# Batched 64 x 64 matmul: four of the casts of b go from VectorE to ScalarE

## The chip, the cores and the metric

The kernel runs on one core of a Trainium2 chip. The core has TensorE (PE in the profile), VectorE (DVE), ScalarE (ACT), GpSimd (POOL) and SyncE (SP), which run their own instruction streams and meet at semaphores, and 16 DMA engines which serve the queues of SyncE (q1), ScalarE (q10) and GpSimd (q0). The metric is the device time of one execution in microseconds.

## The reference

```python
def setup_inputs():
    return {
        "a": np.random.randn(1024, 64, 64).astype(np.float32),
        "b": np.random.randn(1024, 64, 64).astype(np.float32),
    }

def reference(a: np.ndarray, b: np.ndarray) -> np.ndarray:
    return np.matmul(a, b).astype(np.float32)
```

There are 1024 independent products of 64 x 64 matrices in fp32. Each of a, b and the output has 16.8 MB, so a run reads 33.55 MB and writes 16.78 MB of HBM.

## The kernel before, in words

The batch is cut into 16 tiles t of 64 products. A tile of b (`b_sb`, 128 partitions x 16 x 128, fp32) is 1 MB. a is loaded for two tiles at once, as a super-tile s = t // 2. Each tile goes through these steps:

- `load_b(t)` brings the fp32 tile of b to SBUF. Odd tiles are issued by ScalarE, even tiles by SyncE (L97). There are three buffers, so the load of tile t + 3 can only be issued when the cast of tile t has read its buffer. In the loop `load_b(t + 3)` stands in iteration t, just after `cast(t + 1)`.
- `cast(t)` turns the tile into bf16 (`b_bf`, two buffers). This is L173. Tile 0 is cast by ScalarE, tiles 1 to 14 by VectorE, tile 15 in quarters by both (L178, L180).
- a is loaded by `load_a`: three quarters of a super-tile are converted to bf16 by GpSimd's DMA (`a_sb`, L74) and the fourth comes as fp32 through SyncE (`a_raw`, L78). Its transposition is made by VectorE for super-tiles 2 to 5 (`transpose_dve`: L128, with ScalarE casting `a_raw` at L126), and by TensorE for the others (`transpose`: L138, evacuated by ScalarE at L141, after VectorE's `regroup` at L109 and L112).
- `spread(t)` copies the transposed a into a block-diagonal tile (`at_bd`, two buffers) on VectorE: eight copies at L154 or four at L164.
- `multiply(t)` runs 64 matmuls (L218) into two PSUM tiles (`o_ps`, two buffers, one for each half of t). ScalarE copies each half out with four instructions (L206), eight for a tile. For tiles 11 and 13 VectorE takes two of these eight, and for the last tile half of its copies.
- `store(t)` writes the 1 MB of products from GpSimd's queue (L195), for the last two tiles from SyncE's and ScalarE's.

The work is written out by hand under `tc.manual_schedule()`: on each engine the instructions stand in the order of the program text. In iteration t of the main loop that order is: `spread(t + 1)`, `cast(t + 1)`, `load_b(t + 3)`, `load_a` (some iterations), TensorE transposes of the second half (some), `multiply(t)` with its copies, then the regroup or the transposition of a super-tile further on, and the store of tile t - 1. On ScalarE this means, for even t: whatever iteration t - 1 left (copies of t - 1, the cast of `a_raw` or transposed copies), then `load_b(t + 3)`, then the copies of product t.

Below, "cast 7" is `cast(7)`, "load b9" is `load_b(9)`, "copies 6" are the copies from PSUM of `multiply(6)`.

Of the kernel before, what the change touches and what calls it, by code (L numbers as in the profile page):

```python
# [13 lines left out]
def kernel(  # L14
# [14 lines left out]
    nc = tc.nc  # L29
# [7 lines left out]
    N_BD = 2  # L37
    HOLD = 2
    ON_DVE = (2, 3, 4, 5)

    a_v = a.rearrange("(s g h) (mp v) k -> s h g mp (v k)", h=4, g=32, v=16)
    b_v = b.rearrange("(t g h) (kp u) n -> t (h kp) g (u n)", h=4, g=16, u=2)
# [27 lines left out]
    def load_a(s):  # L70

        a_sb = a_pool.tile([128, 3, 16, 64], bf16, name="a_sb")
        for h in range(3):
            nc.gpsimd.dma_start(  # L74
                out=a_sb[:, h, :, :].rearrange("p v k -> p (v k)"), in_=a_v[s, h], single_packet=True
            )
        a_raw = a_pool.tile([128, 16, 64], fp32, name="a_raw")
        nc.sync.dma_start(out=a_raw[:].rearrange("p v k -> p (v k)"), in_=a_v[s, 3])  # L78
        a_tiles[s] = a_sb, a_raw
# [53 lines left out]
    def transpose(s, j):  # L133
        a_cols = abf_tiles[s][:].rearrange("p v h k -> p v (h k)").bitcast(fp32)
        for wl in range(2):
            at_ps = t_psum.tile([128, 4, 128], fp32, name="at_ps")
            for vo in range(4):
                nc.tensor.transpose(  # L138
                    at_ps[:, vo, :], a_cols[:, 4 * vo + 2 * j + wl, :], identity[:]
                )  # L140
            nc.scalar.copy(  # L141
                at_tiles[s][:, :, 2 * j + wl, :, :],
                at_ps[:].rearrange("p vo (g mp) -> p g mp vo", mp=4),
            )

    def spread(t):
        bd = bd_tiles[t % N_BD]
        at_sb = at_tiles[t // 2]
        for h in range(4):
            rows = slice(32 * h, 32 * h + 32)  # L150
            if t // 2 in ON_DVE:
                for i in range(2):
# [16 lines left out]
    def cast(t):  # L169
        b_bf = work.tile([128, 16, 128], bf16, name="b_bf")  # L170
        b_sb = b_tiles.pop(t)
        if t < n_t - 1:
            (nc.vector.tensor_copy if t else nc.scalar.copy)(b_bf[:], b_sb[:])  # L173
        else:
            for gq in range(4):
                rows = slice(4 * gq, 4 * gq + 4)
                if gq % 2:
                    nc.vector.tensor_copy(b_bf[:, rows, :], b_sb[:, rows, :])  # L178
                else:
                    nc.scalar.copy(b_bf[:, rows, :], b_sb[:, rows, :])  # L180
        bbf_tiles[t] = b_bf
# [5 lines left out]
    def multiply(t):  # L187
# [20 lines left out]
        for half in range(2):  # L208
# [19 lines left out]
            if not last:  # L228
                copies = [nc.scalar.copy] * 4
                if half and t % 2 and t > 2 * max(ON_DVE):  # L230
                    copies[2:] = [nc.vector.tensor_copy] * 2
# [7 lines left out]
    with tc.manual_schedule():  # L239
# [15 lines left out]
        transpose(0, 1)  # L255
        spread(0)
        cast(0)
        for t in range(n_t):
            s, half = t // 2, t % 2
            if t + 1 < n_t:  # L260
                spread(t + 1)
                cast(t + 1)
            if t + B_AHEAD < n_t:
                load_b(t + B_AHEAD)
            if half == 0 and 0 < s < n_s - 1 - A_AHEAD:
                load_a(s + 1 + A_AHEAD)
            if half == 0 and 0 < s < n_s - 1 and s + 1 not in ON_DVE:
                transpose(s + 1, 1)
            multiply(t)
            if t == 0:  # L270
                regroup(1)
                load_a(A_AHEAD)
                load_a(A_AHEAD + 1)
                transpose(1, 0)
                transpose(1, 1)
            if t and s + 2 in ON_DVE and (half or s):
                for part in [0, 1] if t == 1 else [half]:
                    transpose_dve(s + 2, part)
                if half:
                    a_tiles.pop(s + 2)  # L280
            elif half == 0 and 0 < s and s + 2 < n_s:
                regroup(s + 2)
            elif half == 1 and s + 2 < n_s:
                transpose(s + 2, 0)
            if t >= HOLD - 1:
                store(t - HOLD + 1)
# [32 lines left out]
```

## Time and profile before

| | |
|---|---|
| time, median of 3 runs | 134.24 us (134.1 to 134.47) |
| time of the profiled execution | 134.24 us |
| its span, from first to last instruction | 132.1 us |
| VectorE busy | 100.7 us (76%) |
| ScalarE busy | 89.2 us (68%) |
| TensorE matmul busy | 63.2 us (48%) |
| moved between HBM and SBUF | 381 GB/s over the span |

The page of the profile divides the span into 40 slices of 3.3 us. The rows of tenths give for each slice the busy share of an engine as a digit (9 is 90% or more). A group line names the source line, the engine, the operation, output and input, and the number of instructions, then the busy time and the mean duration in ns, then the idle time of the engine just before them with what ended it. A timeline line gives the start, the duration and the instruction; a bracket tells how long the engine was idle before it and what it waited for. `ACTq` marks the issue of a DMA. In the DMA view an issue line ends with the time from issue to landing, and a queue line gives packets, MB and the share of the 16 engines' time. (The "0.5 KB" of a b load's issue line is not its size; a load has 1 MB.)

### The profile page before, as it was taken

The numbers are of one execution on the slowest core, as the hardware profiler recorded it, in microseconds if no ns is written. First come the engines' busy times: TensorE is split into PE (matmuls) and PEld (weight loads), VectorE is DVE, ScalarE is ACT, GpSimd is POOL, SyncE is SP. The second block draws the span as 40 slices with busy tenths as digits, with TensorE's granted clock in tenths as the row PEclk, the third lists the DMA queues.
The fourth block names the chain that finished last, engine by engine and source line by source line (L and its number), as shares of the span: only waits on it lengthen the run. The fifth ranks groups of instructions, "written<-read, shape, count | busy, mean of one in ns | idle before, by whom it ended". The sixth has DMA issues, their size and how long they took to land.

```text
span 132.1 us, 2719 instructions
## 1 busy us (share of the span) xinstructions
PE 63.2 (48%) x1088; PEld 60.5 (46%) x1088; DVE 100.7 (76%) x150; ACT 89.2 (68%) x159; POOL 32.0 (24%) x43
## 2 busy tenths in 40 slices
PE   0006406990733701909190737359709834677700
PEld 0006306980733701909190737259709734676700
DVE  5930399209999915999989998999999998598730
ACT  2225524999893790583989197929999996728970
POOL 8991000420074000702061302040203040312000
PEclk9999999999686555555555555555995995555555
DMA  3999999999999999999999999999999999999996
GB/s 83 351 336 310 309 313 277 288 301 327 326 305 385 371 308 298 395 385 396 327 282 357 402 395 347 296 326 387 399 392 394 394 392 387 398 399 396 364 324 201
DMA packets 19020, 44.99 MB, mean 341 GB/s; under 512 B 1088, under 2 KB 3136, under 8 KB 19008
## 3 DMA queue, kind: packets, MB, share of 16 engines
q0 software_dynamic: 6832, 20.19, 50.6%
q1 hardware_dynamic: 7120, 14.68, 30.8%
q10 hardware_dynamic: 5056, 9.96, 20.0%
q8 instruction: 8, 0.13, 0.4%
q14 instruction: 4, 0.03, 0.1%
HBM read 33.55 MB, written 16.78 MB: 381 GB/s over the span
## 4 chain that ended last, share of the span: by engine, by line
DMA 37%; DVE 27%; ACT 13%; PE 9%; issue 8%; ACTq 2%; SPq 1%
DMA b_sb<-in_b_dram 31%; DVE at_bd L154 11%; ACT o_sb L206 11%; DMA o_sb<-in_a_dram 6%; DVE b_bf L173 6%; PE o_ps L218 5%; DVE at_bd L164 4%; PE at_ps L138 3%; DVE at_sb L128 3%; DVE a_bf L109 1%; DVE a_bf L112 1%; ACTq L97 1%; ACT a_bf L126 1%; ACT a_bf L106 1%; ACT at_sb L141 1%
## 5 line engine op out<-in xcount | busy, mean ns | idle before, releaser
L206 ACT COPY o_sb<-o_ps 64x512 f32<-64x512 f32 x116 | 67.4, 581 | 19.2 <-PE o_ps L218 16.1
L218 PEld LDWEIGHTS <-at_bd 128*128 128x128 bf16 x1024 | 50.5, 125 | 52.9 <-DVE b_bf L173 44.7
L218 PE MATMUL o_ps<-b_bf,at_bd 128*128 128x64 bf16 x960 | 49.1, 231 | 49.4 <-DVE b_bf L173 42.7
L164 DVE COPY at_bd<-at_sb 32x1024 f32<-32x1024 f32 x32 | 23.2, 724 | 12.7 <-ACT at_sb L141 11.9
L154 DVE COPY at_bd<-at_sb 32x512 f32<-32x512 f32 x64 | 27.9, 436 | 1.3
L195 POOL DMA_DIRECT2D out_dram<-o_sb x14 | 15.5, 1108 | 47.5 <-ACT o_sb L206 30.7
L74 POOL DMA_DIRECT2D a_sb<-in_a_dram x21 | 12.4, 606 | 39.8 <-DVE at_sb L128 26.4
L173 DVE CAST b_bf<-b_sb 128x2048 bf16<-128x2048 f32 x14 | 17.2, 1227 | 6.4 <-DMA b_sb<-in_b_dram 6.0
L138 PE MATMUL at_ps<-identity,a_bf 128*128 128x128 f32 x64 | 11.2, 349 | 11.2 <-ACT a_bf L106 11.2
L138 PEld LDWEIGHTS at_ps<-identity,a_bf 128*128 128x128 f32 x64 | 10.3, 188 | 11.1 <-issue 11.1
L128 DVE STREAM_TRANSPOSE at_sb<-a_sb 128x512 f32<-128x512 f32 x12 | 12.0, 1062 | 0.0
L141 ACT COPY at_sb<-at_ps 128x512 f32<-128x512 f32 x16 | 8.5, 594 | 2.1 <-PE at_ps L138 2.0
L106 ACT CAST a_bf<-o_sb 128x1024 bf16<-128x1024 f32 x2 | 2.1, 1044 | 5.2 <-DMA o_sb<-in_a_dram 5.2
L128 DVE STREAM_TRANSPOSE at_sb<-a_bf 128x512 f32<-128x512 f32 x4 | 4.2, 1053 | 0.7 <-ACT a_bf L126 0.7
L126 ACT CAST a_bf<-a_raw 128x1024 bf16<-128x1024 f32 x4 | 4.2, 1046 | 0.7 <-DMA a_raw<-in_a_dram 0.6
L173 ACT CAST b_bf<-b_sb 128x2048 bf16<-128x2048 f32 x1 | 1.9, 1898 | 3.7 <-DMA b_sb<-in_b_dram 3.7
L206 DVE COPY o_sb<-at_ps 64x256 f32<-64x256 f32 x8 | 3.4, 422 | 1.3 <-PE at_ps L218 1.2
L246 DVE MEMSET at_bd<- 128x4096 f32 x1 | 3.5, 3472 | 0.8 <-issue 0.8
L218 PE MATMUL at_ps<-b_bf,at_bd 128*128 128x64 bf16 x64 | 3.6, 242 | 1.0 <-DVE at_bd L164 1.0
L106 DVE CAST a_bf<-o_sb 128x1024 bf16<-128x1024 f32 x2 | 2.8, 1385 | 1.7 <-DMA o_sb<-in_a_dram 1.7
L206 ACT COPY o_sb<-at_ps 64x256 f32<-64x256 f32 x8 | 2.9, 367 | 0.1
L180 ACT CAST b_bf<-b_sb 128x512 bf16<-128x512 f32 x2 | 1.1, 616 | 2.8 <-DMA b_sb<-in_b_dram 2.8
(16 smaller groups left out, 15.4 us busy)
## 6 DMA issues: line engine op xcount, KB each, us to landing
out_dram<-o_sb POOLq DMA_DIRECT2D x14, 1024.0 KB, 21.1
a_sb<-in_a_dram POOLq DMA_DIRECT2D x21, 256.0 KB, 16.0
a_raw<-in_a_dram SPq DMA_DIRECT2D x7, 512.0 KB, 16.9
o_sb<-in_a_dram SPq DMA_DIRECT2D x2, 512.0 KB, 5.8
o_sb<-in_a_dram ACTq DMA_DIRECT2D x2, 512.0 KB, 7.1
out_dram<-o_sb SPq DMA_DIRECT2D x2, 512.0 KB, 3.6
out_dram<-o_sb SPq DMA_DIRECT2D x2, 256.0 KB, 3.6
out_dram<-o_sb ACTq DMA_DIRECT2D x2, 256.0 KB, 3.1
```

The source lines that it names most:

```text
L74: nc.gpsimd.dma_start(out=a_sb[:, h, :, :].rearrange("p v k -> p (v k)"), in_=a_v[s, h], single_packet=True)
L106: copy(a_bf[:, :, h, :], a_sb[h].rearrange("p (v k) -> p v k", v=16))
L126: nc.scalar.copy(rows, raw[:])
L128: nc.vector.transpose(at_tiles[s][:, h].rearrange("p g w mp vo -> p w vo g mp"), pairs.rearrange("p (vo w kp) -> p w vo kp", vo=4, w=4),)
L138: nc.tensor.transpose(at_ps[:, vo, :], a_cols[:, 4 * vo + 2 * j + wl, :], identity[:])
L141: nc.scalar.copy(at_tiles[s][:, :, 2 * j + wl, :, :], at_ps[:].rearrange("p vo (g mp) -> p g mp vo", mp=4),)
L154: nc.vector.tensor_copy(bd[rows, 8 * i : 8 * i + 8, :, h, :, :].rearrange("p g w mp vo -> p (g w) (mp vo)"), at_sb[block : block + 32, h]. ...
L164: nc.vector.tensor_copy(bd[rows, :, :, h, :, :].rearrange("p g w mp vo -> p (g w) (mp vo)"), at_sb[rows, half].rearrange("p g w mp vo -> p ...
L173: (nc.vector.tensor_copy if t else nc.scalar.copy)(b_bf[:], b_sb[:])
L195: store_queue(t, lo).dma_start(out=o_v[t, :, lo : lo + n, :], in_=o_sb[:, lo : lo + n].rearrange("p gh j wl n -> p (gh j wl n)"),)
L206: copies[2 * par + wl](dst, src)
L218: nc.tensor.matmul(o_ps[:, gl, g % 2, j, :], at_bd[:, j, g, :, u], b_bf[:, g, 64 * u : 64 * u + 64], start=(u == 0), stop=(u == 1),)
```

## The change

ScalarE casts the b tiles 5, 7, 9 and 11 besides tile 0; VectorE casts the other tiles up to 14. The place of `cast` in the program text stays, so on ScalarE's stream the cast of tile t + 1 stands ahead of `load_b(t + 3)` and of the copies of product t, for t = 4, 6, 8 and 10. Buffers, queues and the rest are as before.

```diff
--- before.py
+++ after.py
@@ -37,6 +37,7 @@
     N_BD = 2
     HOLD = 2
     ON_DVE = (2, 3, 4, 5)
+    ON_ACT = (0, 5, 7, 9, 11)
 
     a_v = a.rearrange("(s g h) (mp v) k -> s h g mp (v k)", h=4, g=32, v=16)
     b_v = b.rearrange("(t g h) (kp u) n -> t (h kp) g (u n)", h=4, g=16, u=2)
@@ -170,7 +171,7 @@
         b_bf = work.tile([128, 16, 128], bf16, name="b_bf")
         b_sb = b_tiles.pop(t)
         if t < n_t - 1:
-            (nc.vector.tensor_copy if t else nc.scalar.copy)(b_bf[:], b_sb[:])
+            (nc.scalar.copy if t in ON_ACT else nc.vector.tensor_copy)(b_bf[:], b_sb[:])
         else:
             for gq in range(4):
                 rows = slice(4 * gq, 4 * gq + 4)
```

## The prediction

> **What bounds the kernel now.** b5 means b tile 5, and so on; times are us from the span's start. I read the page first, then ScalarE's and VectorE's timelines, then the DMA view cut to single issues.
>
> ```profile
> DVE  5930399209999915999989998999999998598730
> ACT  2225524999893790583989197929999996728970
> DMA  3999999999999999999999999999999999999996
> ...
> L173 DVE CAST b_bf<-b_sb 128x2048 bf16<-128x2048 f32 x14 | 17.2, 1227 | 6.4 <-DMA b_sb<-in_b_dram 6.0
> ...
> L173 ACT CAST b_bf<-b_sb 128x2048 bf16<-128x2048 f32 x1 | 1.9, 1898 | 3.7 <-DMA b_sb<-in_b_dram 3.7
> ```
>
> From 50 to 112 us VectorE is full, ScalarE has holes until 89, and the DMA engines are full almost throughout: three limits lie close together. One cast takes 1.227 us on VectorE and 1.898 on ScalarE. So by engine time alone the change pays: 4 x 1.227 = 4.9 us off VectorE, 4 x 1.898 = 7.6 onto ScalarE (89.2 to 96.8 of 132.1).
>
> What decides is when the tiles land. The loads of odd tiles are issued by ScalarE (L97). Issue and time to landing, from the DMA view cut to one issue each (first two lines: b7 issued at 52.49, b9 at 66.04; then b11 at 80.16, b13 at 94.00, b15 at 104.84):
>
> ```profile
> b_sb<-in_b_dram ACTq DMA_DIRECT2D x1, 0.5 KB, 16.6
> b_sb<-in_b_dram ACTq DMA_DIRECT2D x1, 0.5 KB, 16.9
> b_sb<-in_b_dram ACTq DMA_DIRECT2D x1, 0.5 KB, 14.7
> b_sb<-in_b_dram ACTq DMA_DIRECT2D x1, 0.5 KB, 15.6
> b_sb<-in_b_dram ACTq DMA_DIRECT2D x1, 0.5 KB, 14.4
> ```
>
> Landings: b7 69.1, b9 82.9, b11 94.9, b13 109.6, b15 119.2; b5 51.3 (35.18 + 16.1). VectorE's casts began at 58.31, 72.37, 86.13 and 97.80 for 5, 7, 9, 11: 3 to 7 us after landing. Now ScalarE around the place of cast 7 and load b9:
>
> ```profile
> 65.98 0.02 ACT L97 MOVE_SHAPE b_sb<-in_b_dram  x1
> 66.04 0.70 ACTq L97 DMA_DIRECT2D b_sb<-in_b_dram  x1
> 66.28 1.05 ACT L126 CAST a_bf<-a_raw 128x1024 bf16<-128x1024 f32 x1
> 67.93 4.74 ACT L206 COPY o_sb<-o_ps 64x512 f32<-64x512 f32 x8 [0.60 <-PE o_ps L218]
> 75.58 4.74 ACT L206 COPY o_sb<-o_ps 64x512 f32<-64x512 f32 x8 [2.91 <-PE o_ps L218]
> ```
>
> b9 was issued at 66.04, 0.09 after VectorE's cast 6 (64.72 + 1.23) released its buffer, three us before b7 landed. The new cast 7 stands before that issue in ScalarE's program. Does a waiting cast hold the issue behind it? Once in this trace, yes:
>
> ```profile
> 35.02 1.05 ACT L126 CAST a_bf<-a_raw 128x1024 bf16<-128x1024 f32 x1 [0.60 <-DMA a_raw<-in_a_dram]
> 35.12 0.02 ACT L97 MOVE_SHAPE b_sb<-in_b_dram  x1
> 35.18 0.70 ACTq L97 DMA_DIRECT2D b_sb<-in_b_dram  x1
> ```
>
> b5's buffer was free from 33.94 (cast 2), but its issue came only once the cast ahead, which waited for its own data, had begun.
>
> Last, a load's delay is not only transfer. ScalarE's ring (q10) in the microsecond from 70, the first that lists it after the issue at 66.04:
>
> ```profile
> q0 software_dynamic: 59, 0.17, 52.8%
> q1 hardware_dynamic: 58, 0.12, 32.4%
> q10 hardware_dynamic: 42, 0.09, 22.1%
> ```
>
> Likewise 52.49 to 56.5 and 80.16 to 84.3: some 4.1 us from issue to first packet. Rings with work get equal packet counts (48 to 50 per us with three rings, 67 with two), and a load is 512 packets of 2 KB.
>
> **The change, part by part.**
>
> *Removed.* Four casts leave VectorE. Cast 5 gives all it promises: spread 5 ends at 58.28, so matmul 5 starts at 58.3 instead of 59.6. The later ones are limited by ScalarE, below.
>
> *Cast 5 on ScalarE.* ScalarE is done with the a_raw cast at 49.6, b5 lands at 51.3, the cast runs to 53.2. Load b7 behind it waits for cast 4 (52.41) anyway, and copies 4 (the evacuation of product 4) start at 54.39. ScalarE's own hole before 54.39 hides it, at no cost; had b5 landed at 54.4 instead, copies 4 would start 1.9 late.
>
> *Cast 7.* Copies 5 now end at 65.0 and a_raw at 66.1, then ScalarE waits for b7 until 69.1 and casts to 71.0. Behind it stand load b9 (66.04 becomes 69.2) and copies 6 (67.93 becomes 71.0, to 75.7). Who waits for those: matmul 7, whose first PSUM half is free at 73.4 against its start at 73.66 before. So VectorE's 1.2 to 2.4 us of lead are used up here, and what is left is a load issued 3.2 us later.
>
> *Cast 9.* b9 lands at 69.2 + 16.9 = 86.1 (own row of before, with three rings again sharing); copies 8 start at 88.0 instead of 82.05, copies 9 end at 97.5 instead of 94.1, and load b11 is issued at 86.2 instead of 80.16.
>
> *Cast 11.* Before, b11 had SyncE's ring empty beside it for part of its transfer. Now b12, issued near 88, shares most of the way, as b14 did with b13; so b13's 15.6 is the nearest row, and b11 lands at X = 86.2 + 15.6 = 101.8 (94.9 before). Bounds: 14.4 and 16.9 for both loads give X = 98.1 to 103.1. ScalarE is free at 98.5 (copies 9, two transposed copies of 0.51), so the landing is what ends last.
>
> *From X to the end.* ScalarE then has cast 11 (1.9), two transposed copies (1.0), copies 10 (4.75), copies 11 (3.6), half a us more, then load b15: X + 11.7 = 113.5, where it was 104.84. VectorE's spread 12 waits for those transposed copies and cast 12 ends near 109, in time. b15's time to land: 14.4 in its own row, where b14 and a store shared the way. Below: 4.1 to the first packet, 1.05 MB at the 400 GB/s of full windows (2.6), 1.4 from last packets to landing, 8.1 in all. I take 11.0, since b14 will be through and one store (256 packets of 4 KB at 67 per us, 4 us) runs beside it. b15 lands at 124.5. From its landing to the end the trace of before has 132.1 - 119.2 = 12.9, and this part is ScalarE's (cast 1.1, copies 14 4.75, copies 15 3.0, last store 3.3 and 0.7), so it stays: 137.4. ScalarE's own work from X + 11.3 (four transposed copies 2.05, copies 12 4.75, copies 13 3.6) makes it free at X + 21.7 = 123.5, so the wait for b15 is 1.0, and with no wait at all the end would still be X + 34.6 = 136.4.
>
> *Queues moved past.* SyncE's loads b8, b10, b12, b14 are released by casts 5, 7, 9, 11: 59.6 to about 54, 73.7 to 71.0, 87.4 to 88.0, 99.1 to 103.7. The first two only queue behind a_raw loads on the same ring. b14 with the 16.1 of its row lands at 119.8, in time for copies 14 at 125; if it took 20 it would cost. GpSimd's stores follow the copies: 8, 9, 10 go at 93, 98, 109.5 instead of 87.08, 94.38, 101.07. By 104 us all that has been issued (30.4 MB of loads, 10.5 MB of stores) is about what the engines can have moved (0.4 MB per us since 2), so I expect the DMA row, full until 124 before, to show a hole near 105.
>
> *Sum.* 132.1 + 8.7 (b15's issue) - 3.4 (its landing) = 137.4. The profiled execution took 134.24, 2.1 more than its span, which is also the median of the runs shown; so 139.5.
>
> *The skill beside it.* The Trainium skill, DMA: Bandwidth & Descriptors, section Rules for kernel authors, advises to issue a transfer early, compute, and wait for its semaphore late. The change does the opposite for the odd tiles: it puts the wait ahead of the next issue. The same page, Anatomy of one DMA, gives about 2.0 us of fixed cost per DMA, against the 4.1 to a first packet here. With 2.0 and about 10.5 of transfer, both loads would take 12.5, X would be 94.3, and the end 128.9, short of the 132.1 of before, so a gain; the 14.4 to 16.9 of the rows decide.
>
> **The rivals.**
>
> *Faster: ScalarE isn't held.* If tiles land before ScalarE reaches their casts, VectorE's 1.23 per odd tile comes through. That needs b7 before 66.1, 3.0 earlier than it lands, and loads of at most 12.5 afterwards. VectorE's and ScalarE's sums give some 2 us by copies 10, but the DMA bytes cap it: in the three windows of 4 us from 120 the engines move 381, 327 and 240 GB/s against 397 before, 0.97 MB or 2.4 us short, half of it the last store's own delay. Price: -1.3, 132.9. For it: VectorE full in the row of tenths. Against: five landing rows.
>
> *Same: the lateness is absorbed.* Total bytes are fixed and DMA is full; if delayed stores merely let loads pass, b15 would land near 119. Price 134.2. Against: stores and loads wait behind the same ScalarE queue, and X + 34.6 exceeds 132.1 for any X over 97.5.
>
> *Slower, milder.* Loads of 14.4 and b15 at 9: X = 98.1, ScalarE's own end 132.7, b15's path 131.7; span 132.7 to 134, time 134.9 to 136.
>
> *Slower, harder.* 16.9 twice and b15 again 14.4: 103.1 + 11.7 + 14.4 + 12.9 = 142.1, time 144.2.
>
> **How the numbers follow.** No change can be told from one within 0.3% (0.4 us). Forecast (137 to 142) 0.58, milder 0.20, harder 0.08, same 0.05, faster 0.09. Range 135.0 to 142.5: it leaves out the faster and same cases and the harder one's far end. Slower 0.86, same 0.05, faster 0.09.
>
> **What would show it.** ScalarE's cast group with four more at about 1.9 us and idle before it ended by the DMA of b_sb (near 2 to 3 us each for 7, 9, 11, under 2 for 5); b9 issued near 69, b11 near 86, b15 near 113; copies 6 near 71; VectorE with holes after 80; a DMA hole near 105. I am wrong if b9 is issued before b7 lands (the queue isn't held), if b9 and b11 take under 13 us, or if ScalarE reaches the casts after the landings.

## The result and the profile after

The changed kernel took 139.26 us (median of 6 runs, 138.93 to 139.87) against 134.11 for the kernel before (6 runs on the same chip). The ratio is 1.0371, with a 95% interval of 1.0351 to 1.0392: slower by 5 us. The prediction was 139.5, with a range of 135.0 to 142.5. The profiled span went from 132.1 to 137.1 us.

In the changed kernel all line numbers are one higher (the cast is L174). Its page has these rows of tenths and these two groups of casts:

```profile
DVE  5920499009999819999999639997709169969650
ACT  3135324999890976979099962999499999699920
DMA  3999999999999999999999999999999999992994
...
L174 ACT CAST b_bf<-b_sb 128x2048 bf16<-128x2048 f32 x5 | 9.5, 1898 | 14.6 <-DMA b_sb<-in_b_dram 14.6
...
L174 DVE CAST b_bf<-b_sb 128x2048 bf16<-128x2048 f32 x10 | 12.5, 1252 | 3.4 <-DMA b_sb<-in_b_dram 3.2
```

The four casts have moved at the price expected (1898 ns each), and VectorE's busy time fell from 100.7 to 95.6 us. But VectorE's row, full from 50 to 112 us before, now has holes. ScalarE stood idle for 14.6 us ahead of its casts, each time until a tile of b landed: 4.4 of this is cast 0 (3.7 in the kernel before), the rest belongs to casts 5, 7, 9 and 11.

ScalarE's timeline shows where they are (start, duration, instruction; in brackets the idle time before it and what ended it):

```profile
64.24 1.05 ACT L127 CAST a_bf<-a_raw 128x1024 bf16<-128x1024 f32 x1
68.70 1.90 ACT L174 CAST b_bf<-b_sb 128x2048 bf16<-128x2048 f32 x1 [3.42 <-DMA b_sb<-in_b_dram]
68.80 0.02 ACT L98 MOVE_SHAPE b_sb<-in_b_dram  x1
68.86 0.71 ACTq L98 DMA_DIRECT2D b_sb<-in_b_dram  x1
70.62 9.49 ACT L207 COPY o_sb<-o_ps 64x512 f32<-64x512 f32 x16
80.14 1.04 ACT L127 CAST a_bf<-a_raw 128x1024 bf16<-128x1024 f32 x1
84.98 1.90 ACT L174 CAST b_bf<-b_sb 128x2048 bf16<-128x2048 f32 x1 [3.80 <-DMA b_sb<-in_b_dram]
85.06 0.02 ACT L98 MOVE_SHAPE b_sb<-in_b_dram  x1
85.11 0.70 ACTq L98 DMA_DIRECT2D b_sb<-in_b_dram  x1
86.90 9.50 ACT L207 COPY o_sb<-o_ps 64x512 f32<-64x512 f32 x16
96.42 1.08 ACT L142 COPY at_sb<-at_ps 128x512 f32<-128x512 f32 x2
99.75 1.90 ACT L174 CAST b_bf<-b_sb 128x2048 bf16<-128x2048 f32 x1 [2.25 <-DMA b_sb<-in_b_dram]
99.85 0.02 ACT L98 MOVE_SHAPE b_sb<-in_b_dram  x1
99.91 0.70 ACTq L98 DMA_DIRECT2D b_sb<-in_b_dram  x1
```

This is a loop. ScalarE waits until b7 has landed, and 0.16 us after cast 7 begins it issues load b9. Then it waits until b9 has landed, and issues load b11; then b11, and load b13. Before, each of these loads was issued while the tile ahead of it was still on its way. The chain of work that ended last (start, duration, what) says the same: one load after another, with nearly nothing between them.

```profile
68.80 0.02 ACT b_sb L98
68.83 0.03 issue
68.86 16.05 DMA b_sb<-in_b_dram
84.90 0.02 issue
...
85.06 0.02 ACT b_sb L98
85.08 0.03 issue
85.11 14.56 DMA b_sb<-in_b_dram
99.67 0.02 issue
```

The share of b loads in that chain rose from 31% to 53% of the span.

### The profile page after: what moved, and what is told of

The parts are those of the page before. It is cut to its first block, busy times and chain, and to the rows that moved or that the text cites. A ratio compares the mean times of both kernels' runs of the same rounds, so it can differ in the third digit from the quotient of the medians.

```text
span 137.1 us, 2722 instructions
## 1 busy us (share of the span) xinstructions
PE 62.6 (46%) x1088; PEld 60.2 (44%) x1088; DVE 95.6 (70%) x146; ACT 96.6 (70%) x163; POOL 32.4 (24%) x43
## 4 chain that ended last, share of the span: by engine, by line
DMA 59%; DVE 16%; ACT 9%; PE 5%; issue 4%; ACTq 1%; SPq 1%; DVEq 0%
DMA b_sb<-in_b_dram 53%; DVE at_bd L165 8%; ACT o_sb L207 7%; DMA o_sb<-in_a_dram 6%; DVE o_sb L207 4%; DVE b_bf L174 3%; PE at_ps L139 3%; PE at_ps L219 1%; PE o_ps L219 1%; ACT at_sb L142 1%; ACT a_bf L107 1%; ACTq L98 1%; DVE a_bf L113 1%; ACTq L92 0%; SPq L79 0%
## 5 line engine op out<-in xcount | busy, mean ns | idle before, releaser
L219 PEld LDWEIGHTS <-at_bd 128*128 128x128 bf16 x1024 | 49.7, 122 | 58.7 <-DVE b_bf L174 23.5
L219 PE MATMUL o_ps<-b_bf,at_bd 128*128 128x64 bf16 x960 | 48.5, 229 | 55.2 <-ACT o_sb L207 22.1
L165 DVE COPY at_bd<-at_sb 32x1024 f32<-32x1024 f32 x32 | 22.7, 708 | 16.6 <-ACT at_sb L142 15.9
L196 POOL DMA_DIRECT2D out_dram<-o_sb x14 | 16.1, 1152 | 54.6 <-ACT o_sb L207 40.7
L174 ACT CAST b_bf<-b_sb 128x2048 bf16<-128x2048 f32 x5 | 9.5, 1898 | 14.6 <-DMA b_sb<-in_b_dram 14.6
L139 PE MATMUL at_ps<-identity,a_bf 128*128 128x128 f32 x64 | 11.8, 361 | 11.2 <-ACT a_bf L107 11.2
L139 PEld LDWEIGHTS at_ps<-identity,a_bf 128*128 128x128 f32 x64 | 10.8, 196 | 11.1 <-issue 11.1
L174 DVE CAST b_bf<-b_sb 128x2048 bf16<-128x2048 f32 x10 | 12.5, 1252 | 3.4 <-DMA b_sb<-in_b_dram 3.2
L207 DVE COPY o_sb<-o_ps 64x512 f32<-64x512 f32 x4 | 2.8, 690 | 5.4 <-ACT o_sb L207 5.4
## 6 DMA issues: line engine op xcount, KB each, us to landing
a_sb<-in_a_dram POOLq DMA_DIRECT2D x21, 256.0 KB, 15.6
```

The costliest lines, as they stand in the source:

```text
L139: nc.tensor.transpose(at_ps[:, vo, :], a_cols[:, 4 * vo + 2 * j + wl, :], identity[:])
L165: nc.vector.tensor_copy(bd[rows, :, :, h, :, :].rearrange("p g w mp vo -> p (g w) (mp vo)"), at_sb[rows, half].rearrange("p g w mp vo -> p ...
L174: (nc.scalar.copy if t in ON_ACT else nc.vector.tensor_copy)(b_bf[:], b_sb[:])
L196: store_queue(t, lo).dma_start(out=o_v[t, :, lo : lo + n, :], in_=o_sb[:, lo : lo + n].rearrange("p gh j wl n -> p (gh j wl n)"),)
L207: copies[2 * par + wl](dst, src)
L219: nc.tensor.matmul(o_ps[:, gl, g % 2, j, :], at_bd[:, j, g, :, u], b_bf[:, g, 64 * u : 64 * u + 64], start=(u == 0), stop=(u == 1),)
```

## The experiments

Every kernel was timed against the kernel before, in the same session on one chip. There were four sessions, so the median of before differs a little: 134.11 for the changed kernel, 134.46 for e1 to e4, 134.18 for e5 to e8 and 134.35 for e9 to e11. Landing times are from the DMA view cut to one issue each. In the code excerpts below, constants and small helper functions are written in place.

| run | what | us | ratio to before, 95% interval |
|---|---|---|---|
| changed kernel | casts 5, 7, 9, 11 on ScalarE | 139.26 | 1.0371 (1.0351 to 1.0392) |
| e1 | only the waits | 138.64 | 1.0319 (1.0267 to 1.0370) |
| e2 | only ScalarE's time | 135.32 | 1.0068 (1.0039 to 1.0098) |
| e3 | load issued ahead of the cast | 133.75 | 0.9959 (0.9934 to 0.9983) |
| e4 | cast 5 alone | 133.80 | 0.9960 (0.9943 to 0.9978) |
| e5 | the waits, behind the issue | 134.37 | 1.0003 (0.9984 to 1.0023) |
| e6 | loads issued a little later, no wait | 134.59 | 1.0028 (1.0008 to 1.0049) |
| e7 | changed kernel, four b buffers | 134.77 | 1.0040 (1.0023 to 1.0057) |
| e8 | kernel before, four b buffers | 135.02 | 1.0053 (1.0033 to 1.0073) |
| e9 | loads issued 3.6 us later, no wait | 137.28 | 1.0218 (1.0191 to 1.0245) |
| e10 | casts 5 and 7 | 134.13 | 0.9993 (0.9976 to 1.0009) |
| e11 | issue first, casts 5, 7, 9 | 133.78 | 0.9958 (0.9940 to 0.9977) |

### Is it the wait or the work? (e1, e2)

e1, against the kernel before (VectorE makes its casts as before, so the output stays whole):

```diff
                 spread(t + 1)
+                if t + 1 in (5, 7, 9, 11):
+                    nc.scalar.copy(warm[:, 1:2], b_tiles[t + 1][:, 15, 127:128])
                 cast(t + 1)
             if t + B_AHEAD < n_t:
                 load_b(t + B_AHEAD)
```

> The kernel before, with VectorE doing all its casts; at the four places where the change puts a cast, ScalarE only copies one column of b5, b7, b9, b11 to a scratch column, so it waits for the landing there and works for some 0.2 us. Theory (ScalarE's queue is held until the odd tile has landed, and the next load and the copies stand behind): nearly the whole loss comes back, b9 issued near 69 and b11 near 85 as in the changed kernel, time 137.5 to 140. Rival (the loss is ScalarE's 4 x 1.9 us of work, when it is full from 89 on): 134.1 within 0.5.

e2 has in the same place a copy that waits for no b tile:

```diff
+                if t + 1 in (5, 7, 9, 11):
+                    nc.scalar.copy(junk[:], identity[:].unsqueeze(1).to_broadcast([128, 16, 128]))
```

> The kernel before, with VectorE doing all its casts; at the same four places ScalarE writes a scratch tile of 128 x 2048 bf16 from a tile that is there since the start, some 1.9 us, without waiting for any b. Theory (held queue): three of the four lie in ScalarE's holes, the fourth (near 95) pushes full work by up to 1.9, so 134.1 to 136. Rival (ScalarE's work is the loss): 138 to 140.

Measured: the waits alone cost 3.2%, the work alone 0.7%, both inside what the held queue foresaw. e2's copies took 1.9 us each, the work of the casts. In e1 ScalarE works only 0.19 us at each place, and its timeline still has the loop:

```profile
69.45 0.19 ACT L185 COPY warm<-b_sb 128x1 f32<-128x1 f32 x1 [2.77 <-DMA b_sb<-in_b_dram]
69.55 0.02 ACT L98 MOVE_SHAPE b_sb<-in_b_dram  x1
69.61 0.70 ACTq L98 DMA_DIRECT2D b_sb<-in_b_dram  x1
...
85.19 0.19 ACT L185 COPY warm<-b_sb 128x1 f32<-128x1 f32 x1 [4.29 <-DMA b_sb<-in_b_dram]
...
99.85 0.19 ACT L185 COPY warm<-b_sb 128x1 f32<-128x1 f32 x1 [3.14 <-DMA b_sb<-in_b_dram]
```

So the waits at these places are most of the loss, and ScalarE's 7.6 us of work is not. The changed kernel's ratio lies 0.5% above e1's, but the intervals overlap, so that difference is not told apart.

### Take the issue out of the wait (e3, e5)

e3 leaves all four casts on ScalarE and turns two calls round:

```diff
                 spread(t + 1)
+                first = t + 1 in ON_ACT and t + B_AHEAD < n_t
+                if first:
+                    load_b(t + B_AHEAD)
                 cast(t + 1)
-            if t + B_AHEAD < n_t:
+            if t + B_AHEAD < n_t and not first:
                 load_b(t + B_AHEAD)
```

> The changed kernel with load b(t+3) ahead of cast t+1 on ScalarE, for casts 5, 7, 9, 11. Theory: b9 is issued near 65 and b11 near 77 instead of 68.9 and 85.1, cast 9 begins near 82 and cast 11 near 94, copies 10 near 97, time 133.7 to 135.7: most of the loss goes. Rival one (copies held behind the wait are the loss, not the late issue): 137 or more. Rival two (ScalarE's work): 138 to 139.5.

```profile
65.49 0.72 ACTq L98 DMA_DIRECT2D b_sb<-in_b_dram  x1
69.53 1.90 ACT L174 CAST b_bf<-b_sb 128x2048 bf16<-128x2048 f32 x1 [3.19 <-DMA b_sb<-in_b_dram]
71.45 7.71 ACT L207 COPY o_sb<-o_ps 64x512 f32<-64x512 f32 x13
78.65 0.02 ACT L98 MOVE_SHAPE b_sb<-in_b_dram  x1
78.71 0.71 ACTq L98 DMA_DIRECT2D b_sb<-in_b_dram  x1
...
82.46 1.90 ACT L174 CAST b_bf<-b_sb 128x2048 bf16<-128x2048 f32 x1 [0.45 <-DMA b_sb<-in_b_dram]
...
94.86 1.91 ACT L174 CAST b_bf<-b_sb 128x2048 bf16<-128x2048 f32 x1
```

ScalarE still waits 3.19 us for b7, and copies 6 still begin late (71.45). But load b9 is out at 65.49, so the wait at cast 9 shrinks to 0.45 us and at cast 11 there is none. The whole loss is gone, and the kernel is 0.4% faster than before. (The execution in this trace took 134.80 us, the longest of ten; the median is 133.75.) So neither held copies nor ScalarE's work, both still there, explains the loss.

e5 is the counterpart on the kernel before: the one-column copy of e1, behind `load_b(t + B_AHEAD)` instead of ahead of it.

> As the run that only waits (VectorE casts everything, ScalarE copies one column of b5, b7, b9, b11), but the waiting copy stands behind load b(t+3): the copies of the products are still held, the loads no more. If the late issue is the loss: b9 issued near 66, b11 near 80.5, copies 6 held by some 1.6 us, copies 8 and 10 by about 1, time 134.5 to 136. If the held copies are the loss: 137 to 139.

It costs nothing: 134.37 us (1.0003), just under the range of 134.5 to 136. ScalarE waits 1.94 us for b7 and 1.65 for b9, and not at all for b11 (e1: 2.77, 4.29, 3.14). The waits of e1 for b9 and b11 were so long because their loads had been issued late.

### Late loads without any wait on ScalarE (e6, e9)

Both are the kernel before, with loads b9, b11, b13 moved behind copies of the same iteration, e6 behind the first half and e9 behind the second:

```diff
-            if t + B_AHEAD < n_t:
+            if t + B_AHEAD < n_t and t not in (6, 8, 10):
                 load_b(t + B_AHEAD)
...
                 evacuate(o_ps, 4 * half, 4, copies)
+                if half == 0 and t in (6, 8, 10):    # e9: half == 1
+                    load_b(t + B_AHEAD)
```

> The kernel before, without any wait on ScalarE; only the loads b9, b11, b13 are issued later, behind the copies of the first half of products 6, 8 and 10, so b9 goes near 69.5 instead of 66.0. Nothing else is held. If the late issue is the loss: b9 lands near 86, b11 is issued near 85 and lands near 99, b13 is issued near 101, VectorE's casts 9 to 13 wait for DMA, time 136 to 139. If the held copies are the loss: 134 to 135.

> As the run with late issues alone, but the loads b9, b11, b13 stand behind all eight copies of products 6, 8 and 10 (the first half was a delay of only 0.7 to 1.8 us): b9 near 70, b11 near 83, b13 near 97.5, that is 3 to 4 us late each, as much as a single held cast gives, but not tied to the landing before. If a fixed lateness of that size costs what the changed kernel lost: 137 to 139. If the loss needs the loop (each issue waits for the landing before, so that lateness adds up): 134.5 to 136.5.

e6 came out at 134.59 us (1.0028), in the range of the held copies and not in the 136 to 139 of the late issue. But its dose was small: the loads went at 67.87, 81.01 and 94.69, only 1.8, 0.9 and 0.7 us later than before, where I had expected 69.5 for b9. ScalarE issued each load without waiting for the four copies ahead of it to run: the first of them began at 67.73, 80.87 and 95.45. So e6 does not decide between the two.

e9's loads went at 69.59, 83.73 and 97.66, 3.6 us late each, and it took 137.28 (1.0218). VectorE's casts 10 to 13, now waiting for DMA at 11 and 13:

```profile
92.39 1.23 DVE L174 CAST b_bf<-b_sb 128x2048 bf16<-128x2048 f32 x1
98.58 1.23 DVE L174 CAST b_bf<-b_sb 128x2048 bf16<-128x2048 f32 x1 [1.10 <-DMA b_sb<-in_b_dram]
104.43 1.23 DVE L174 CAST b_bf<-b_sb 128x2048 bf16<-128x2048 f32 x1
113.40 1.23 DVE L174 CAST b_bf<-b_sb 128x2048 bf16<-128x2048 f32 x1 [3.20 <-DMA b_sb<-in_b_dram]
```

b13 landed at 113.4 (109.6 before; 113.0 in the changed kernel). So late loads alone bring back 2.9 us (2.2%). I had put a fixed lateness of this size at either 137 to 139 or 134.5 to 136.5; the first held, so most of the loss does not need the loop. What the loop does is bring the lateness about, and let it grow: b9, b11, b13 are issued 2.8, 5.0 and 5.9 us late in the changed kernel. The further 1% from e9 to e1 goes with b11 and b13 being later still (85.33 and 99.98) and with copies that stand behind the wait; these two were not told apart.

### One or two casts only (e4, e10)

```diff
-    ON_ACT = (0, 5, 7, 9, 11)
+    ON_ACT = (0, 5)       # e10: (0, 5, 7)
```

> The changed kernel with cast 5 alone moved (tiles 0 and 5 on ScalarE). Theory: the cast lies in ScalarE's hole and the load behind it waits for cast 4 anyway, so 133.7 to 134.5, with matmul 5 starting 1.3 us earlier. Rival (each cast costs its part of the 5 us): 135.4.

> The changed kernel with only tiles 5 and 7 (and 0) on ScalarE: one link of the loop, b9 issued near 69 instead of 66. Loop theory: b9 lands near 85, about when VectorE comes to its cast, and nothing is added after, so 133.6 to 134.8. If each held cast costs its share: near 136.

Cast 5 alone is a small gain (0.9960): load b7 behind it waits for cast 4 anyway (52.65, before 52.49), and later work starts earlier (copies 7 at 74.13 instead of 75.58). In e10, ScalarE waits 3.5 us at cast 7 and load b9 goes at 68.86, as in the changed kernel. Yet nothing is lost: b9 lands at 84.9, VectorE comes to it at 85.90, and load b11 goes at 77.89, earlier than before (80.16). So one late load of 2.8 us is paid by slack. The loss comes with casts 9 and 11, when b11 and b13 are late too; no run split these two.

### How much could be gained? (e7, e8, e11)

e7 is the changed kernel and e8 the kernel before, both with `B_AHEAD = 4` (and b3 loaded at the start of iteration 0).

> The changed kernel with four buffers for the fp32 tiles of b instead of three (loads one tile further ahead). Theory: load b9 is then issued in iteration 5, ahead of cast 7, and the odd tiles have landed when ScalarE reaches their casts; ScalarE no longer idles for them and VectorE's relief comes through as far as the DMA engines let it: 132.5 to 134.3. If the casts themselves cost, 137 or more.

> The kernel before with four buffers for the fp32 tiles of b: the control for the run with four buffers and the casts on ScalarE. The loads waited for little before (6.0 us on VectorE in three places, 2.8 on ScalarE near the end), so 133.3 to 134.8; the difference to the run with the casts on ScalarE is what those casts buy when nothing holds the queue.

Both expectations were missed, in the same direction: 134.77 and 135.02, slower than the kernel before. In e7 ScalarE does not wait for b at 7, 9 or 11, and all copies are done by 123.1, five us earlier than before. The windows of 4 us from 120 (busy time of PE, PEld, DVE, ACT, POOL, then the clock, DMA share and GB/s) show what is left:

```profile
120.00:124.00 4.00, 1.24 (x24) 1.08 (x21) 2.96 (x7) 1.84 (x6) 0.00 (x0) 0.81 1.03 372
124.00:128.00 4.00, 0.00 (x0) 0.00 (x0) 0.00 (x0) 0.00 (x0) 0.00 (x0) 0.61 1.02 341
128.00:132.00 4.00, 0.00 (x0) 0.00 (x0) 0.00 (x0) 0.00 (x0) 0.00 (x0) 0.50 0.61 206
```

No engine computes after 124, and the DMA engines are full for four microseconds more. In this run their work sets the end, and faster computing would not have shortened it. (Why the span is then still 0.9 us over that of the kernel before is open.) e7 against e8 is what the casts on ScalarE buy where nothing holds the queue: 0.25 us, within the intervals.

e11 is e3 with cast 11 on VectorE.

> Load ahead of the cast, and tiles 5, 7, 9 on ScalarE; cast 11, which stands where ScalarE is full, goes back to VectorE. The DMA engines' work sets a floor: with four buffers all copies were done by 122 and the run still took 134.8. So 133.2 to 134.2, little or nothing under 133.8.

133.78, 0.4% faster than before. e3, e4 and e11 beat both kernels by the same small amount. A floor set by DMA fits e4 and e11, whose DMA share from 124 to 128 is 1.01 and 1.03 (0.94 in the kernel before). In e3's trace it is 0.74, so there the floor is not shown.

## Why the prediction was right, point by point

**The held queue** was the mechanism, and its single row of evidence (the issue at 35.18 behind a cast waiting to 35.02) held up: in e1 the wait alone brings back most of the loss, in e3 removing the issue from behind it takes all of it away. One reading beside it was loose: q10 is listed from 66 to 69 too, with 52, 20 and 3 packets, but these are the last of b7, which landed at 69.1; none of b9 comes before 70.

**The steps up to X** came out nearly as written. Cast 5: hidden, as e4 shows. Load b9 at 69.2, measured 68.86; copies 6 at 71.0, measured 70.62; load b11 at 86.2, measured 85.11; landing of b11 (X) at 101.8, measured 99.7. The two loads took 16.0 and 14.6 us where the rows of b9 and b13 gave 16.9 and 15.6, so X came 2.1 us earlier than written.

**The term that failed is b15.** I put its issue at X + 11.7 and 11.0 us to its landing at 124.5, and let its landing set the end. It was issued at 110.33 (X + 10.6) and landed 9.8 us later, at 120.1; ScalarE reached its cast at 122.06 without waiting. What set the end is what I had as second, the engines' own work from X on, but I put it at X + 34.6, which with the measured X is 134.3. The span was 137.1, so this term was 2.8 too small. VectorE's last rows of the changed kernel show why:

```profile
119.39 1.48 DVE L174 CAST b_bf<-b_sb 128x2048 bf16<-128x2048 f32 x1
122.19 1.39 DVE L207 COPY o_sb<-o_ps 64x512 f32<-64x512 f32 x2 [1.31 <-ACT o_sb L207]
123.61 3.09 DVE L165 COPY at_bd<-at_sb 32x1024 f32<-32x1024 f32 x4
126.73 0.77 DVE L179 CAST b_bf<-b_sb 128x512 bf16<-128x512 f32 x2
128.68 3.48 DVE L207 COPY o_sb<-at_ps 64x256 f32<-64x256 f32 x8 [1.19 <-PE at_ps L219]
```

VectorE's two copies of product 13 stand ahead of spread 15, and begin only when ScalarE's six copies of the same product have ended (122.15), though the matmuls were done by about 120. From there VectorE needs 10.0 us to its end, in both kernels. ScalarE needs 8.9 when it does not wait for b15, and 11.7 in the kernel before, where it waited 2.77; that wait had hidden VectorE's path. So VectorE, not ScalarE, ends last (132.16 against 131.03; before 126.56 against 128.24), and the span ends 4.9 us after it, where the tail of before had 3.9 after ScalarE. I had carried ScalarE's tail over as it was. The two misses, X 2.1 too late and the tail from ScalarE's cast of b15 on 2.1 too short (12.9, measured 15.0), cancel: 137.4 against 137.1. The loss and its mechanism were foreseen; that the number came so close is luck.

**The hole in DMA** came, but 20 us later than I said. The windows of the changed kernel:

```profile
104.00:108.00 4.00, 2.57 (x46) 2.46 (x46) 2.65 (x4) 3.89 (x8) 0.47 (x1) 0.50 1.03 371
...
120.00:124.00 4.00, 1.37 (x38) 1.36 (x39) 2.64 (x4) 3.92 (x8) 0.00 (x0) 0.87 0.85 311
124.00:128.00 4.00, 2.83 (x54) 2.67 (x52) 3.37 (x6) 3.86 (x7) 1.35 (x1) 0.50 0.50 170
```

Near 105 the engines are full (share 1.03). The hole is at 124 to 128 (0.50). My balance of bytes at 104 took 0.4 MB per us; with the 381 GB/s that the kernel before had over its span, 38.9 of the 40.9 MB issued would have moved, and work was left. That a hole comes once stores follow late copies was right: the store of product 13 was issued only at 124.14, when all loads had landed.

**The rivals.** "Faster" needs landings before ScalarE arrives; the landings stayed where the rows had them. When the order is turned round (e3), a gain is there, but some 0.6 us (0.41% of 134.46), under half of the 1.3 allowed. "The lateness is absorbed" is true of one link (e10), not of three.

**The skill's fixed cost.** The estimate from the 2.0 us of the Trainium skill's DMA: Bandwidth & Descriptors, section Anatomy of one DMA, would have made the two loads 12.5 us and the change a gain. That section gives its figure for DMAs of GpSimd's path, and these loads are issued by ScalarE, so it was no figure for them. They took 16.0 and 14.6 here, so the 12.5 that the "faster" case also asked for was not reached; the measured rows decide. The advice of the page's section Rules for kernel authors (issue early, wait late) is what e3 restores: 133.75 us, against 139.26 with the wait ahead of the issue.

## What to carry to other kernels

Moving an instruction to a less busy engine also moves its wait. If that engine issues DMAs too, look at what stands behind the new wait in its stream: a load whose issue sits behind a wait for the load before it makes a loop, with the time to landing as its period (here 14.6 to 16.0 us for two tiles of work that had taken 14). Put the issue ahead of the wait, as e3 does; then compare the landing times, not the busy times, with the places where the data is wanted.

## What the runs showed of the hardware that I had not expected

- Some 4.1 us pass from the issue of a 1 MB load to its first packets while other rings are busy, a quarter of its time to landing. Rings with work get equal numbers of packets (48 each in the microsecond from 79 in the kernel before), not of bytes (0.20 MB for GpSimd's ring, 0.10 for each of the others).
- ScalarE issues a load ahead of a few instructions that stand before it and have not begun: in e6 the load behind four copies went at 67.87, with the first of them begun at 67.73. More copies hold it back: in e9, behind eight, load b13 went at 97.66, 1.94 us after the first copy began (95.72) and with four still to begin, though the matmuls of that product were done by 95.72. A wait ahead holds it until the waiting instruction begins (68.70 and 68.86 in the changed kernel).
- More prefetch made the run slower by 0.4 to 0.5% with either kernel (e7, e8), though the work on the engines ended earlier.
